# Another order of the SSD stage in a two-layer encoder: taps, softplus, SiLUs and SSD items

## The chip, the cores and the metric

One NeuronCore of one Trainium2 chip runs the whole program. The metric is the device time of one execution in microseconds (us); the time before is the median of three runs, 1902.2 us (1900.9 to 1903.83).

## What is computed

The reference is a trunk of two layers on a sequence of 1024 positions with 1024 channels, float32. Layer 0 is dilated attention, layer 1 a bidirectional Mamba-2 mixer (SSD). Each sub-layer is RMSNorm, shift and scale from `c`, the mixer, a gate and a residual. The part that matters here is the mixer of layer 1, cut to its core (32 heads of 64, 8 groups, state 128, convolution over 5 positions, chunks of 128):

```python
proj = h @ w_in
z, xbc, dt_raw = split(proj)                 # 2048, 4096, 2 x 32
xbc = silu(conv5(xbc) + conv_b)              # depthwise, five taps
xs, bm, cm = split(xbc)                      # 2048, 8 x 128, 8 x 128
dt = softplus(dt_raw + dt_bias)
a = -exp(a_log)
y_f = ssd_scan(xs, dt[:, :, 0], a[0], bm, cm)
y_b = flip(ssd_scan(flip(xs), flip(dt[:, :, 1]), a[1], flip(bm), flip(cm)))
y = (y_f + y_b + xs * d_skip) * silu(z)
return rms_norm(y, norm_w) @ w_out
```

In `ssd_scan`, with `acs` the cumulative sum of `dt * a` in a chunk, the output of a chunk is `(C B^T * decay) (x dt)`, with `decay = exp(acs_l - acs_s)` below the diagonal, plus `exp(acs) * (C state)`, and the states go from chunk to chunk.

## The kernel before

Everything lies transposed: channels on the 128 partitions, positions along the free axis. A float32 product is made of three matmuls on rounded halves (lines 376 to 378). For that each weight tile is loaded by SP into `wraw` (four buffers, line 349), ScalarE rounds it to `whi` (line 271) and VectorE, or GpSimd for a while, subtracts to get `wlo` (line 272, `split`).

The work of layer 1 goes by eight groups g of four heads. A group has six **blocks** of 128 output channels: x0, x1, B, C (convolved) and z0, z1 (gates). A block is eight dense **steps** (`dense`), one per 128 input channels, six matmuls of 512 columns each; it fills two of four accumulator banks `acc`. So a block can start once the banks of the block before the last are free. `block_order` gives the order: x0, z0, x1, B, C, z1 in groups 1 to 6, x0, x1, B, C, z0, z1 in groups 0 and 7. In group 0, x0 and x1 are computed by `start1` together with dt, and B goes to banks `a2`, `a3`.

After a convolved block ScalarE evacuates the middle tap with the bias (line 1322) and VectorE adds the other four taps straight from the banks, two instructions each (line 1330). The banks are free after the last tap. Then comes a SiLU over the tile (line 1334). A gate is evacuated by SiLU or by a copy with a SiLU later (lines 1342, 1347). `group_dense` writes a group's dense steps as a list, with taps and SiLUs inserted behind given steps; the keys of `late` are (position of the block, step).

`dt_items` is the softplus of group 0's head: `tok` transposes dt and takes exp; `ratio`, seven times `series` and `end` compute log1p by a series on VectorE; `rows` makes the cumulative sums by matmuls with triangles and writes them to DRAM (`acsd`); `back` transposes them back and makes `dtdec` (the weights of x for the states). Between `tok` and `back` the splits are GpSimd's.

`ssd_items` gives a group's SSD work, for chunks c of 128 positions: `A1` transposes x0, x1 and B of a chunk (banks `a0`, two of them) and copies them out on ScalarE; `A2` scales x by `dtdec` (xd, line 1415), makes the state products and carries the states; `B0` loads a chunk's `acs` from DRAM into one of four buffers; `B1` makes the exponents E (line 1440), the product cb of B and C, and exp on ScalarE; `M` combines them to the matrices (lines 1462 to 1467); `B2` multiplies and adds x times d (yt, line 1482), and GpSimd multiplies by the gate. B1 of chunk 7 to M of chunk 0 is called the B phase below, the A2 the A phase.

`layer1` joins the lists. A group's SSD items may start at its `cut`, some entries behind the SiLU of B; what follows, up to the next group's cut, is the main list, and `balance` puts the SSD items between its entries so that the estimated VectorE work (fourth number of an entry) keeps up with the estimated TensorE work (third number). `weave` spreads one list over another by its first number. The items of group 7 are woven into its last dense steps and the first 14 steps of the output projection (`out1`).

Of the kernel before, what the change touches and what calls it, by code (L numbers as in the profile page):

```python
# [91 lines left out]
class Trunk:  # L92
# [1097 lines left out]
    def layer1(self, tail):  # L1190
        nc, io = self.nc, self.io
        self.grp, self.ready = {}, {}
        g0 = self.group_dense(0)
        weave(g0[0], tail)
        self.phase("w2")
        self.cv = self.u("cv", [P, 32, 6])
        nc.sync.dma_start(self.cv, io["cv"])
        self.sv = self.u("sv", [P, 34])
        nc.sync.dma_start(self.sv, io["sv"][:, :34])
        self.alog = self.big()[:, :64]  # L1200
        nc.sync.dma_start(self.alog, io["sv"][:, 34:98])
        self.yd = self.scratch("yd", [14, P, S])
        for _, f in g0[1]:
            f()
        main = [g0[2]] + [self.group_dense(g) for g in range(1, 8)]
        cut = [next(i for i, it in enumerate(m) if it[1] is self.ready[g]) + 4 for g, m in enumerate(main)]
        cut[0] += 3
        weave(main[0][:cut[0]], self.dt_items())
        for g in range(7):
            balance(main[g][cut[g]:] + main[g + 1][:cut[g + 1]], self.ssd_items(g))  # L1210
        return main[7][cut[7]:], self.ssd_items(7)
# [6 lines left out]
    def dt_items(self):  # L1218
# [5 lines left out]
        C = 8  # L1224
# [31 lines left out]
        def series(k):  # L1256
            nc.vector.scalar_tensor_tensor(st["q"], st["q"], 1.0 / k, st["w"], op0=OP.add, op1=OP.mult)
# [34 lines left out]
        def back():  # L1292
            self.lo_engine = nc.vector
            p = self.bank("a0", [P, C, 64], 2)
            for c in range(C):
# [7 lines left out]
            nc.vector.tensor_mul(self.dtdec, x, self.dt)  # L1303

        wait = (lambda: None)
        return ([(100, tok), (300, ratio)] + [(200, lambda k=k: series(k)) for k in range(15, 1, -2)]
                + [(300, end), (3800, wait), (100, rows), (1200, wait), (100, back), (3000, wait)])

    def group_dense(self, g):

# [43 lines left out]
        tiles, late, evacs = {}, {}, {}  # L1354
        for pos, m in enumerate(order):
            name = names[m]
            if m < 4:
                e, taps, silu = conv(name, 4 * g + m)
                for i, tp in enumerate(taps):
                    late.setdefault((2, 3 + i) if g == m == 0 else (3 if g == 0 and m == 1 else pos + 1, (0, 1, 3, 5)[i]),  # L1360
                                    []).append(tp)
                if mixed:
                    when = (5, 6) if m == 3 else (5, 0)
                else:
                    when = (5, 0) if m == 3 else (4, 0 if g else 3)
                late.setdefault(when, []).append(silu)
                if m == 2:
                    self.ready[g] = silu[1]
            else:
                e, silu = gate(name, m == 5 or not mixed)  # L1370
                if mixed and m == 4:
                    late.setdefault((5, 1), []).append(silu)
            evacs[m] = e
            banks = ("a2", "a3") if g == 0 and m == 2 else None
            if g or m > 1:
                tiles[pos] = self.dense(self.wb["in1"] + 2 * (6 * g + pos), e, banks)
# [9 lines left out]
    def ssd_items(self, g):  # L1386
# [3 lines left out]
        C = 8  # L1390
# [3 lines left out]
        def ck(c):  # L1394
            return slice(P * c, P * c + P)
# [4 lines left out]
        def A1(c):  # L1400
            p = self.bank("a0", [P, 3, P], 2)
            for i, n in enumerate(("x0", "x1", "B")):
                nc.tensor.transpose(p[:, i], st[n][:, ck(c)], ident)  # L1403
            x = xt[c] = self.u("xt", [P, 4, 64], F32, 8)
            nc.scalar.copy(x.rearrange("p h q -> p (h q)"), p[:, :2].rearrange("p i q -> p (i q)"))
            b = bt[c] = self.u("bt", [P, P], F32, 8)
            nc.scalar.copy(b, p[:, 2])
# [20 lines left out]
        def B0(c):  # L1428
            a = live["a", c] = self.u("acs", [P, 2, 4, P], F32, 4)
            nc.sync.dma_start(a, self.acsd[c, :, hs][None].to_broadcast([P, 2, 4, P]))  # L1430
# [60 lines left out]
                    nc.gpsimd.dma_start(self.yd[2 * g + r], st[f"z{r}"])  # L1491

        def a1(c):
            return 200, lambda: A1(c), 0.35, 0.3

        def a2(j):
            return 900, lambda: A2(j), 0.9, 2.3

        items = []
        for j in range(C // 2):  # L1500
            items += [a1(j), a1(C - 1 - j)]
            if j:
                items.append(a2(j - 1))
        items.append((1, lambda: B0(C - 1), 0, 0))
        items += [a2(j) for j in range(C // 2 - 1, C)]
        if g == 7:
            items.append((1500, lambda: None, 0, 0))
        for c in range(C - 1, -1, -1):
            items.append((900, lambda c=c: B1(c), 0.25, 1.6))
            if c < C - 2:  # L1510
                items.append((500, lambda c=c: B2(c + 2), 1.7, 0.6))
            if c:
                items.append((1, lambda c=c: B0(c - 1), 0, 0))
            items.append((1150, lambda c=c: M(c), 0, 3.0))
        items += [(500, lambda: B2(1), 1.7, 0.6), (900, lambda: None, 0, 1.5), (500, lambda: B2(0), 1.7, 0.6)]
        return items

# [270 lines left out]
```

## Time and profile before

| | |
|---|---|
| median of three runs | 1902.2 us (1900.9 to 1903.83) |
| profiled execution | 1903.41 us, span 1901.6 us |
| TensorE (PE) busy | 1790.2 us, 94% |
| VectorE (DVE) busy | 1428.1 us, 75% |
| ScalarE (ACT) busy | 955.5 us, 50% |
| GpSimd (POOL) busy | 330.1 us, 17% |
| mean granted TensorE clock | 0.976 |

The profile is one execution. A wait is the idle time of an engine just before an instruction, put down to what ended it. A busy TensorE isn't one at its peak, since matmuls are pipelined. The SSD stage with its head lies between about 937 and 1745 us of the span; what goes on before and after it (attention, the projections) is touched by no part of the change.

### The profile page before, as it was taken

What the parts mean: (1) busy time and instruction counts of PE and PEld (TensorE: products, weight loads), DVE (VectorE), ACT (ScalarE), POOL (GpSimd) and SP (SyncE); (2) the same over time, 40 slices, a digit from 0 to 9 for tenths busy, and PEclk for the clock granted to TensorE, in tenths of its full rate; (3) what the DMA queues carried; (4) which work ended last, traced back from release to release, by engine and by line L of the source; (5) the groups of instructions that cost most, each with busy time, mean ns of one, the idle gap of its engine ahead of it and who ended that gap; (6) DMA issues with size and microseconds to landing.
All of it is one profiled execution on the core that took longest, in us unless ns stands there. A gap on an engine that the chain in (4) does not pass through costs nothing.

```text
span 1901.6 us, 28474 instructions
## 1 busy us (share of the span) xinstructions
PE 1790.2 (94%) x10050; PEld 1462.0 (77%) x10050; DVE 1428.1 (75%) x3220; ACT 955.5 (50%) x2095; POOL 330.1 (17%) x492
## 2 busy tenths in 40 slices
PE   5899999999999999999979999999999999888997
PEld 3678788777788887779868887878787877666787
DVE  8867568667664665566778898989898989878875
ACT  5454445444454545444435656464655555465632
POOL 4611122112211311000100101010101000233310
PEclk7899999999999999999989999999999999988998
DMA  6242234222311321355113232424232323244643
GB/s 254 87 130 81 81 107 134 85 86 83 105 52 54 81 60 49 91 188 169 63 45 99 85 100 78 100 78 101 78 110 80 106 83 91 89 129 127 199 155 101
DMA packets 99733, 193.65 MB, mean 102 GB/s; under 512 B 15624, under 2 KB 23048, under 8 KB 99592
## 3 DMA queue, kind: packets, MB, share of 16 engines
q1 hardware_dynamic: 86600, 167.32, 28.3%
q0 software_dynamic: 12288, 23.86, 4.5%
q8 instruction: 79, 1.29, 0.3%
q10 hardware_dynamic: 704, 0.66, 0.1%
q14 instruction: 62, 0.51, 0.1%
HBM read 169.00 MB, written 16.48 MB: 98 GB/s over the span
## 4 chain that ended last, share of the span: by engine, by line
PE 40%; DVE 7%; ACT 5%; issue 3%; DMA 2%; SPq 0%; DVEq 0%; POOL 0%; ACTq 0%; POOLq 0%
PE acc L376 8%; PE acc L378 7%; PE acc L377 7%; PE a L1478 3%; PE a L1416 2%; PE a L1002 2%; PE a L1000 2%; PE a L1001 2%; PE acc L1002 2%; PE acc L1001 1%; PE acc L1000 1%; DVE big L1330 1%; DVE wlo L272 1%; PE a L1403 1%; DMA acs<-acsd 1%
## 5 line engine op out<-in xcount | busy, mean ns | idle before, releaser
L376 PE MATMUL acc<-big,whi 128*128 128x512 f32 (+1 forms) x1520 | 632.7, 416 | 36.2 <-DVE big L1330 23.9
L377 PE MATMUL acc<-big,whi 128*128 128x512 f32 (+1 forms) x1520 | 597.3, 393 | 4.0 <-DVE big L294 4.0
L378 PE MATMUL acc<-big,wlo 128*128 128x512 f32 (+1 forms) x1520 | 597.2, 393 | 0.3 <-DVE wlo L272 0.3
L376 PEld LDWEIGHTS acc<-big,whi 128*128 128x128 f32 x1520 | 289.0, 190 | 103.7 <-issue 31.5
L378 PEld LDWEIGHTS acc<-big,wlo 128*128 128x128 f32 x1520 | 288.6, 190 | 64.8 <-DVE wlo L272 1.1
L377 PEld LDWEIGHTS acc<-big,whi 128*128 128x128 f32 x1520 | 290.1, 191 | 55.3 <-DVE big L294 7.5
L272 DVE TENSOR_TENSOR wlo<-wraw,whi 128x512 fp32r<-128x512 f32 (+1 forms) x298 | 216.8, 732 | 82.3 <-ACT whi L271 78.9
L271 ACT CAST whi<-wraw 128x512 fp32r<-128x512 f32 (+1 forms) x302 | 180.9, 611 | 86.1 <-PE a L1001 29.7
L695 ACT ACTIVATE sm<-sm,nb 128x256 f32<-128x256 f32 (+1 forms) x192 | 89.3, 466 | 198.3 <-DVE nb L693 195.7
L1448 ACT ACTIVATE E<-E,nacb 128x128 f32<-128x128 f32 x256 | 81.8, 391 | 200.2 <-DVE E L1440 200.2
L1486 POOL TENSOR_TENSOR big<-big,yt 128x128 f32<-128x128 f32 x128 | 68.0, 552 | 602.5 <-DVE yt L1482 547.5
L1330 DVE SCALAR_TENSOR_TENSOR big<-acc,cv,big 128x512 f32<-128x512 f32 (+1 forms) x248 | 170.9, 742 | 0.9 <-ACT big L1322 0.9
L706 DVE COPY pt<-a 128x512 f32<-128x512 f32 (+1 forms) x96 | 57.6, 600 | 76.5 <-PE a L704 76.5
L690 DVE CUSTOM_DVE_ANT_0 sm<-a,cst 128x256 f32<-128x256 f32 (+1 forms) x192 | 65.0, 376 | 62.4 <-PE a L685 62.0
L1001 PE MATMUL acc<-big,whi 128*128 128x512 f32 x224 | 91.4, 408 | 9.7 <-DVE big L1553 7.2
L1000 PE MATMUL a<-big,whi 128*128 128x256 f32 (+1 forms) x304 | 100.1, 329 | 0.0
L1002 PE MATMUL a<-big,wlo 128*128 128x256 f32 (+1 forms) x304 | 98.7, 325 | 0.7 <-DVE wlo L272 0.7
L1001 PE MATMUL a<-big,whi 128*128 128x256 f32 (+1 forms) x304 | 98.5, 324 | 0.0
L1002 PE MATMUL acc<-big,wlo 128*128 128x512 f32 x224 | 91.8, 410 | 4.6 <-DVE wlo L272 4.4
L1000 PE MATMUL acc<-big,whi 128*128 128x512 f32 x224 | 92.7, 414 | 1.2 <-ACT big L271 1.2
L592 POOL DMA_DIRECT2D rt<-kT x92 | 50.4, 561 | 249.4 <-ACT kT L532 149.9
L1462 DVE SCALAR_TENSOR_TENSOR W<-cb,dt,W 128x128 f32<-128x128 f32 x256 | 82.7, 379 | 7.3 <-ACT W L1450 6.6
(254 smaller groups left out, 3149.0 us busy)
## 6 DMA issues: line engine op xcount, KB each, us to landing
wraw<-in_win SPq DMA_DIRECT2D x186, 256.0 KB
acs<-acsd SPq DMA_DIRECT2D x64, 512.0 KB
wraw<-in_wout SPq DMA_DIRECT2D x112, 256.0 KB
big<-in_modw SPq DMA_DIRECT2D x48, 512.0 KB
yd<-big POOLq DMA_DIRECT2D x14, 512.0 KB, 3.5
big<-yd SPq DMA_DIRECT2D x28, 256.0 KB
vT<-mix POOLq DMA_DIRECT2D x20, 256.0 KB, 5.0
big<-in_xT SPq DMA_DIRECT2D x8, 512.0 KB
```

The lines of the kernel that those rows point to most:

```text
L271: self.nc.scalar.copy(dst_hi, src)
L272: self.late.append((lambda: self.lo_engine.tensor_sub(dst_lo, src, dst_hi.bitcast(F32)), tile))
L376: mm(o, hi[:, cols], x_[:, t0:t0 + n], start=first, stop=False, **kw)
L377: mm(o, hi[:, cols], x_[:, H2 + t0:H2 + t0 + n], start=False, stop=False, **kw)
L378: mm(o, lo[:, cols], x_[:, t0:t0 + n], start=False, stop=last, **kw)
L695: nc.scalar.activation(sm[:, h, :W], sm[:, h, :W], AF.Exp, bias=nb[:, h:h + 1], scale=0.125, accum_out=stat[:, h, 1, i:i + 1])
L1000: mm(o, hi[:, c], x[:, t:t + n], start=kt == 0 and (n == H2 or m % 2 == 0), stop=False, **kw)
L1001: mm(o, hi[:, c], x[:, H2 + t:H2 + t + n], start=False, stop=False, **kw)
L1002: mm(o, lo[:, c], x[:, t:t + n], start=False, stop=kt == nkt - 1, **kw)
L1330: nc.vector.scalar_tensor_tensor(y[:, lo:hi], a[:, lo + o:hi + o], w[:, cv, k:k + 1], y[:, lo:hi], op0=OP.mult, op1=OP.add)
L1448: nc.scalar.activation(E[:, h], E[:, h], AF.Exp, bias=self.nacb[:, c, 4 * g + h:4 * g + h + 1])
L1462: nc.vector.scalar_tensor_tensor(W[:, h], cb[:, 1], self.dt[:, c, hh:hh + 1], W[:, h], op0=OP.mult, op1=OP.add)
```

## The change

It changes the order of instructions in layer 1 and nothing else.

- `layer1`: a group's SSD items may start 7 entries behind B's SiLU, not 4 (7 in group 0).
- `dt_items`: other first numbers, by which the softplus parts are spread over group 0's dense steps.
- `group_dense`: the four taps of a block go behind steps 0, 1, 2, 3 of the next block, not 0, 1, 3, 5. In group 0 x0's taps go behind steps 0 and 1 of B, x1's behind steps 5 to 7 of B and 0 of C, C's behind steps 0 to 3 of z0, B's behind steps 4 to 7 of z0. Group 0's SiLUs move to step 0 of z1. z0's SiLU in groups 1 to 6 moves from step 1 to step 6 of z1, that of C from 6 to 5.
- `ssd_items`: A1 counts 0.8 instead of 0.3 us of VectorE; the loads B0 of chunks 7 and 6 are issued together ahead of the last A2, and each later one comes behind M, two chunks ahead of its use instead of one.

```diff
         main = [g0[2]] + [self.group_dense(g) for g in range(1, 8)]
-        cut = [next(i for i, it in enumerate(m) if it[1] is self.ready[g]) + 4 for g, m in enumerate(main)]
-        cut[0] += 3
+        cut = [next(i for i, it in enumerate(m) if it[1] is self.ready[g]) + 7 for g, m in enumerate(main)]
...
-        return ([(100, tok), (300, ratio)] + [(200, lambda k=k: series(k)) for k in range(15, 1, -2)]
-                + [(300, end), (3800, wait), (100, rows), (1200, wait), (100, back), (3000, wait)])
+        return ([(200, wait), (100, tok), (100, ratio), (500, wait)]
+                + [(80, lambda k=k: series(k)) for k in range(15, 1, -2)]
+                + [(100, end), (300, wait), (100, rows), (200, wait), (100, back), (700, wait)])
...
-                    late.setdefault((2, 3 + i) if g == m == 0 else (3 if g == 0 and m == 1 else pos + 1, (0, 1, 3, 5)[i]),
-                                    []).append(tp)
+                    if g:
+                        when = pos + 1, i
+                    else:
+                        when = ((2, i // 2), (2 + i // 3, (5, 6, 7, 0)[i]), (4, 4 + i), (4, i))[m]
+                    late.setdefault(when, []).append(tp)
                 if mixed:
-                    when = (5, 6) if m == 3 else (5, 0)
+                    when = (5, 5) if m == 3 else (5, 0)
                 else:
-                    when = (5, 0) if m == 3 else (4, 0 if g else 3)
+                    when = (5, 1) if m == 3 else (4, 0) if g else (5, 0)
...
                 if mixed and m == 4:
-                    late.setdefault((5, 1), []).append(silu)
+                    late.setdefault((5, 6), []).append(silu)
...
-            return 200, lambda: A1(c), 0.35, 0.3
+            return 200, lambda: A1(c), 0.35, 0.8
...
-        items.append((1, lambda: B0(C - 1), 0, 0))
+        items.append((1, lambda: (B0(C - 1), B0(C - 2)), 0, 0))
...
-            if c:
-                items.append((1, lambda c=c: B0(c - 1), 0, 0))
             items.append((1150, lambda c=c: M(c), 0, 3.0))
+            if c > 1:
+                items.append((1, lambda c=c: B0(c - 2), 0, 0))
```

Some lines have other numbers in the changed kernel: from 1208 to 1305 they are one less, from there to 1359 the same, and from the middle of `group_dense` on, the SSD items among it, three more (1403 is 1406, 1440 is 1443).

VectorE at the head of the stage, before. big_8986, big_8984 and big_8985 are tiles of the softplus, big_8958 is x0, and acc_8578 and acc_8579 are its banks:

```order
L272 TENSOR_TENSOR wlo_8919<-wraw_8601,whi_8918 128x512
L1240 COPY big_8986<-a_1636_8975 128x512
L1241 TENSOR_SCALAR big_8984<-big_8986 128x512
L1242 SCALAR_TENSOR_TENSOR big_8984<-big_8986 128x512
L1250 TENSOR_SCALAR big_8985<-big_8984 128x512
L1251 RECIPROCAL big_8985<-big_8985 128x512
L1252 TENSOR_TENSOR big_8984<-big_8984,big_8985 128x512
L1253 TENSOR_TENSOR big_8985<-big_8984 128x512
L1254 TENSOR_SCALAR big_8985<-big_8985 128x512
L1257 SCALAR_TENSOR_TENSOR big_8985<-big_8985 128x512 x7
L1330 SCALAR_TENSOR_TENSOR big_8958<-acc_8578,cv_8789,big_8958 128x512
L1330 SCALAR_TENSOR_TENSOR big_8958<-acc_8579,cv_8789,big_8958 128x510
```

The same place now, from the last tap of x0 on; big_8955 with acc_8580 is x1, and the softplus tiles are big_9012, big_9010 and big_9011:

```order
L1330 SCALAR_TENSOR_TENSOR big_8958<-acc_8578,cv_8789,big_8958 128x510
L1330 SCALAR_TENSOR_TENSOR big_8958<-acc_8579,cv_8789,big_8958 128x512
L272 TENSOR_TENSOR wlo_8980<-wraw_8606,whi_8979 128x512
L1239 COPY big_9012<-a_1639_9001 128x512
L1240 TENSOR_SCALAR big_9010<-big_9012 128x512
L1241 SCALAR_TENSOR_TENSOR big_9010<-big_9012 128x512
L1249 TENSOR_SCALAR big_9011<-big_9010 128x512
L1250 RECIPROCAL big_9011<-big_9011 128x512
L1251 TENSOR_TENSOR big_9010<-big_9010,big_9011 128x512
L1252 TENSOR_TENSOR big_9011<-big_9010 128x512
L1253 TENSOR_SCALAR big_9011<-big_9011 128x512
L1330 SCALAR_TENSOR_TENSOR big_8955<-acc_8580,cv_8789,big_8955 128x512
```

All eight taps of x0 stand ahead of the softplus, and x1's eight between its `ratio` and its `series`; before, x0's were behind the series and x1's behind `end`. On TensorE the matmuls of `rows` follow 20 dense steps of this list, 14 before.

VectorE in the main list of group 1, where x1 of group 2 (big_10748) gets its last taps, before:

```order
L1330 SCALAR_TENSOR_TENSOR big_10748<-acc_10594,cv_8789,big_10748 128x511
L1330 SCALAR_TENSOR_TENSOR big_10748<-acc_10595,cv_8789,big_10748 128x512
L1440 SCALAR_TENSOR_TENSOR E_10840<-acs_10788,delta_8965 128x128 x4
L1446 TENSOR_TENSOR cb_10848<-a_1972_10846,cst_71 128x256
L1482 SCALAR_TENSOR_TENSOR yt_10872<-big_9594,sv_8791,a_1974_10859 128x128
L1482 SCALAR_TENSOR_TENSOR yt_10872<-big_9871,sv_8791,a_1974_10859 128x128
L1462 SCALAR_TENSOR_TENSOR W_10841<-cb_10848,dt_8962,W_10841 128x128 x4
L1464 TENSOR_TENSOR E_10840<-E_10840,W_10841 128x512
L1467 TENSOR_TENSOR acs_10788<-acs_10788,big_10145 128x1024
L1330 SCALAR_TENSOR_TENSOR big_10748<-acc_10594,cv_8789,big_10748 128x510
```

And now:

```order
L1330 SCALAR_TENSOR_TENSOR big_10748<-acc_10594,cv_8789,big_10748 128x510
L1330 SCALAR_TENSOR_TENSOR big_10748<-acc_10595,cv_8789,big_10748 128x512
L272 TENSOR_TENSOR wlo_10843<-wraw_10605,whi_10842 128x512
L1443 SCALAR_TENSOR_TENSOR E_10862<-acs_10751,delta_8965 128x128 x4
L1449 TENSOR_TENSOR cb_10870<-a_1976_10868,cst_71 128x256
L1485 SCALAR_TENSOR_TENSOR yt_10894<-big_9535,sv_8791,a_1978_10881 128x128
L1485 SCALAR_TENSOR_TENSOR yt_10894<-big_9820,sv_8791,a_1978_10881 128x128
L1465 SCALAR_TENSOR_TENSOR W_10863<-cb_10870,dt_8962,W_10863 128x128 x4
L1467 TENSOR_TENSOR E_10862<-E_10862,W_10863 128x512
L1470 TENSOR_TENSOR acs_10751<-acs_10751,big_10107 128x1024
L1330 SCALAR_TENSOR_TENSOR big_10905<-acc_10753,cv_8789,big_10905 128x512
```

The last taps of x1 came behind B1 and M of chunk 2; now those of chunk 2 come behind all of x1's taps, and the next taps are B's (big_10905).

SP's queue where group 7's SSD items begin, before; acs_15829 is the load of chunk 7, acs_16014 that of chunk 6, `yd` are loads for the output projection:

```order
L1430 DMA acs_15829<-acsd 128x2x512
L1530 DMA big_15850<-yd 128x512
L349 DMA wraw_15861<-in_wout 128x512
L1530 DMA big_15880<-yd 128x512
L1530 DMA big_15922<-yd 128x512
L349 DMA wraw_15938<-in_wout 128x512
L1530 DMA big_15971<-yd 128x512
L349 DMA wraw_15979<-in_wout 128x512
L349 DMA wraw_15984<-in_wout 128x512
L1430 DMA acs_16014<-acsd 128x2x512
```

And now:

```order
L1533 DMA big_15837<-yd 128x512
L349 DMA wraw_15847<-in_wout 128x512
L1433 DMA acs_15855<-acsd 128x2x512
L1433 DMA acs_15857<-acsd 128x2x512
L1533 DMA big_15860<-yd 128x512
L1533 DMA big_15902<-yd 128x512
L349 DMA wraw_15929<-in_wout 128x512
L1533 DMA big_15973<-yd 128x512
L349 DMA wraw_15981<-in_wout 128x512
L349 DMA wraw_15986<-in_wout 128x512
```

The load of chunk 6 has moved up past three weight loads, to that of chunk 7, which stands one weight load later.

## Rows read from the trace of the kernel before

**Rows 1.** Busy time by stretch: us of PE, PEld, DVE, ACT, POOL, clock, DMA share, GB/s
```profile
987.00:1080.00 93.00, 92.53 (x552) 76.23 (x550) 77.63 (x168) 53.89 (x124) 6.87 (x15) 1.00 0.29 83
1173.00:1266.00 93.00, 89.56 (x532) 73.23 (x532) 81.72 (x175) 52.44 (x123) 8.81 (x19) 1.00 0.33 91
1266.00:1360.00 94.00, 91.12 (x532) 74.38 (x532) 81.29 (x175) 51.91 (x120) 8.58 (x19) 0.98 0.33 90
```
**Rows 2.** Timeline of TensorE, 946 to 992 us: start, us, instruction, idle before
```profile
948.04 0.39 PE L378 MATMUL a<-big,wlo 128*128 128x512 f32 x1
959.97 0.76 PE L376 MATMUL acc<-big,whi 128*128 128x512 f32 x1 [11.54 <-DVE big L1330]
...
965.65 0.39 PE L376 MATMUL acc<-big,whi 128*128 128x512 f32 x1
...
968.38 0.39 PE L376 MATMUL acc<-big,whi 128*128 128x512 f32 x1
...
988.45 0.99 PE L1403 MATMUL a<-cst,big 128*128 128x128 f32 x6 [0.47 <-ACT bt L1407]
```
**Rows 3.** Timeline of VectorE, 938 to 962 us
```profile
938.72 0.69 DVE L1240 COPY big<-a 128x512 f32<-128x512 f32 x1 [5.14 <-PE a L1236]
...
946.94 6.16 DVE L1257 SCALAR_TENSOR_TENSOR big<-big 128x512 f32<-128x512 f32 x7
953.01 1.40 DVE L1330 SCALAR_TENSOR_TENSOR big<-acc,cv,big 128x512 f32<-128x512 f32 x2
954.33 0.68 DVE L1261 SCALAR_TENSOR_TENSOR big<-big,big 128x512 f32<-128x512 f32 x1
...
956.45 5.35 DVE L1330 SCALAR_TENSOR_TENSOR big<-acc,cv,big 128x512 f32<-128x512 f32 x8
```
**Rows 4.** Timeline of ScalarE, 936 to 942 us
```profile
937.28 2.76 ACT L1322 ACTIVATE big<-acc,cv 128x512 f32<-128x512 f32 x4
```
**Rows 5.** Busy time by short stretches, with the granted clock
```profile
953.40:963.40 10.00, 3.43 (x9) 2.74 (x10) 9.86 (x16) 0.00 (x0) 0.00 (x0) 0.51 0.00 1
...
1243.20:1250.00 6.80, 6.80 (x48) 5.62 (x49) 5.87 (x14) 4.43 (x11) 0.89 (x2) 1.00 0.13 41
...
1629.20:1632.50 3.30, 3.30 (x9) 2.58 (x10) 3.28 (x7) 2.06 (x3) 1.94 (x4) 0.55 0.27 109
```
**Rows 6.** Waits of TensorE, 1173 to 1266 us: total, times, longest
```profile
PE acc L376 <- DVE big L1330: 1.5, 1, 1.5
PE a L1403 <- ACT bt L1407: 1.2, 1, 1.2
PE a L1403 <- ACT big L1334: 0.3, 1, 0.3
```
**Rows 7.** Waits of TensorE, 1545 to 1634 us
```profile
PE acc L376 <- DVE big L1330: 4.7, 3, 1.7
PE a L1478 <- issue: 2.8, 1, 2.8
```
**Rows 8.** Busy time, 1600 to 1630 us
```profile
1600.00:1630.00 30.00, 23.78 (x184) 19.38 (x183) 28.84 (x68) 19.91 (x45) 4.84 (x11) 0.98 0.26 69
```
**Rows 9.** Waits of VectorE, 1634 to 1745 us
```profile
DVE E L1440 <- DMA acs<-acsd: 6.6, 1, 6.6
```
**Rows 10.** Timeline of SP's queue, 1600 to 1760 us
```profile
1633.99 0.67 SPq L1430 DMA_DIRECT2D acs<-acsd  x1
...
1642.40 0.33 SPq L349 DMA_DIRECT2D wraw<-in_wout  x1
...
1663.71 11.73 SPq L349 DMA_DIRECT2D wraw<-in_wout  x2
1675.49 0.43 SPq L1430 DMA_DIRECT2D acs<-acsd  x1
```
**Rows 11.** Timeline of VectorE in a steady group, 1244 to 1254 us
```profile
1244.17 1.13 DVE L1440 SCALAR_TENSOR_TENSOR E<-acs,delta 128x128 f32<-128x128 f32 x4
1245.22 0.41 DVE L1446 TENSOR_TENSOR cb<-a,cst 128x256 f32<-128x256 f32 x1
...
1250.32 1.13 DVE L1462 SCALAR_TENSOR_TENSOR W<-cb,dt,W 128x128 f32<-128x128 f32 x4
...
1252.10 1.22 DVE L1467 TENSOR_TENSOR acs<-acs,big 128x1024 f32<-128x1024 f32 x1
```
**Rows 12.** Timeline of VectorE, 950.3 to 951.6 us: one step of the series
```profile
949.84 1.80 DVE L1257 SCALAR_TENSOR_TENSOR big<-big 128x512 f32<-128x512 f32 x1
```

## The prediction

> **What bounds the kernel now.** I looked first at the busy time by stage. TensorE is the bound: between 987 and 1080 us it worked 92.53 of 93 us, from 1173 to 1266 89.56 of 93, while VectorE had 81.72 [rows 1]. So the only gains to be had are TensorE's waits and the stretches in which its clock was at the lower of its two levels, and I went through the SSD stage wait by wait.
>
> At its head stands the largest. TensorE ended the B block of group 0 at 948.3 and started C at 959.97, 11.54 us later, released by a tap on VectorE [rows 2]. The C block needs the two accumulators of x0, and these come free with x0's taps. VectorE had meanwhile been in the softplus: it copied dt at 938.72, began the series of seven steps at 946.94 and ended them at 953.0; then two taps, the softplus end at 954.33, and the other taps from 956.45 [rows 3]. Yet x0 had been evacuated since 940.04 (four evacuations, from 937.28 on for 2.76 us) [rows 4]. The idle time had a second price: from 953.4 to 963.4 the granted clock was 0.51, which is the 1.2 GHz level, and 3.43 us of that were worked [rows 5], so 1.7 us were lost after the restart.
>
> In the steady groups TensorE waits 3.0 us per group: 1.5 for a tap ahead of a dense block, 1.2 + 0.3 for ScalarE at the transposes A1 [rows 6]. One group has 1.6 us more TensorE time (91.12 against 89.56) at a granted clock of 0.98 [rows 1]. Group 6 waits 4.7 for taps and 2.8 at an SSD matmul [rows 7], but VectorE is busy 28.84 of the 30 us from 1600 to 1630 [rows 8]: there it is the bound. In the last group VectorE itself stood still for 6.6 us, for a load of acs [rows 9]; SP issued the load before it at 1633.99, this one at 1675.49, after a weight load that had held the queue for 11.73 us from 1663.71 [rows 10].
>
> **The change part by part.** The sum goes against the profiled execution, 1903.4 us, of which 1901.6 are span. It lies 1.2 above the median of the runs.
>
> *Head.* Gone: 11.5 of waiting and 1.7 of half rate, 13.2. Now x0's eight tap instructions start at 940.0; eight take 5.3 us (956.45 to 961.7) [rows 3], so they end at 945.3, before B ends at 948.3: C doesn't wait. What is late next is the softplus. After a split of 0.6 its first part takes 8.2 (938.72 to 946.94), to 954.2; x1's taps 5.3, to 959.5; the series 6.1, to 965.6; the end 2.1 (954.33 to 956.45), to 967.7 [rows 3]. TensorE has C done at 948.3 + 8 steps of 1.37 (twelve matmuls in 2.73 us, 965.65 to 968.38) [rows 2] = 959.2. z0 waits 0.3 for x1's taps. By the new order the prefix matmuls of `rows` come after 20 dense steps instead of 14, that is four steps into z0, at 965.0; they need the softplus end, so they wait 2.7. A wait of 1.5 us at 1243 was followed by a granted clock of 1.00, one of 2.8 at 1627.9 by 0.55 over 3.3 us [rows 5, 7]. 2.7 is nearest to the latter, so I take one such stretch, 1.7 us. New: 0.3 + 2.7 + 1.7 = 4.7. Queued behind that wait on TensorE are the rest of z0 and z1; nothing else needs it soon, since dtdec is due only at the first A2, 14 dense steps on. Of the splits of weights, one that GpSimd did is now VectorE's (the 0.6). Head: **-8.5**, with ends at -11 (no loss of clock, and the wait 1.1 shorter) and -5 (the wait 2 longer, the stretch at the lower clock twice as long).
>
> The Trainium skill's "TensorE: Matmul & The Clock Gate", section "HAM oscillation — how this bites in real kernels", has the clock fall only after an idle gap longer than a length that it names, and 2.7 is below that; by it the new cost would be 3.0 and the head -10.2. The wait of 2.8 in the rows was below it too and the clock fell, so I stay with the rows.
>
> *Groups 1 to 5.* All five get the same new order. The wait at the transposes shrinks: A1 now comes four dense steps behind the three SiLUs, and z0's SiLU is out of the way. Four A1 in a row still share two banks; in group 0, with ScalarE free, they cost 0.47 [rows 2]. The wait at the tap: x1's last taps stood behind M of chunk 2; now B1, the yt and M of chunk 2 come after them. That takes 1.5 + 0.5 + 2.9 = 4.9 us of VectorE work (1244.17 to 1245.6, one yt pair, 1250.32 to 1253.23 [rows 11]) from ahead of the block start, against 2 dense steps less of cover (2.7, since B1 of chunk 7 comes after step 8 of the next group instead of after step 6). 1.5 + 2.7 - 4.9 is below 0: no wait. But the 2.7 of cover are missing behind that point: VectorE comes to M of chunk 1, and to the xd products of the next A2, with less slack, and TensorE waits there. Ends: 0 and 3.3 (the 2.7 and a split of 0.6); I take 1.0, between 0 and the 1.5 at which a tap is late now. Gone are five waits of 1.5 for taps, five of 1.5 at the transposes, and 1.6 of clock, 16.6; new are 5 x 0.5 and 5 x 1.0. Groups 1 to 5: **-9.1**, ends -14 and +2.4.
>
> *Group 0* has no wait now except that 0.47 [rows 2]; its SSD items begin seven dense steps later and its B phase has the fewest steps of all, 28: **+2.0**, ends 0 and 3.3.
>
> *Group 6.* VectorE has the same work in about as many steps (30 from B1 of chunk 7 to the last B2, 29 before): **0**, ends -5 and +3.
>
> *Last group.* B0 of chunk 6 is issued together with that of chunk 7, three weight loads earlier in SP's queue than now, and that of chunk 7 one later: both behind the weight load that SP issued at 1642.40, ahead of the one that held it from 1663.71 [rows 10]. So the 6.6 us go; VectorE then meets one split and one prep earlier (1.1). The other loads of acs are at most one weight load earlier, and the four buffers still cover them. VectorE is the bound there, so its gain is TensorE's. **-5.5**, ends 0 and -8. The two dense steps that go from this stage to group 6 cost the same in either place.
>
> Softplus, SiLUs, loads and matmuls are as many as before; the 200 and 80 in the lists are weights, not work. Sum: -8.5 - 9.1 + 2.0 + 0 - 5.5 = -21.1, so 1882.3 against 1903.4, and 1.2 less against the median: **1881 us**.
>
> **Rivals.**
> *The arrears eat the groups.* B phases that VectorE can't finish in 28 to 32 steps put waits of 3.0 and more back into each group. For it: by the prices above the phase has 59 us of VectorE work (8 x 1.5 of B1, 8 x 2.9 of M, 6 x 0.5 of yt, 12 pairs of taps at 1.3, 8 splits at 0.6) against 32 steps, 44 us, and less than half of a group's 24 us of SSD matmuls (89.56 - 48 x 1.37); against it: VectorE idles in the A phase, 81.72 of 93 us busy in the whole group [rows 1]. Then groups 1 to 5 give nothing: -8.5 + 0 + 2 - 5.5 = -12, 1890.
> *TensorE alone bounds.* VectorE's slack suffices everywhere, group 6 included: -11 - 14 - 5 - 8 = -38, 1864. For it: VectorE's 81.72 of 93; against it: group 6's 28.84 of 30.
> *GpSimd holds the series up.* One of the seven series steps took 1.80 us instead of 0.7, beside a split on GpSimd [rows 12]. Until `back` all splits run there, and two more may fall beside the series: 2 x 1.1 more waiting at `rows`, and 1.7 more at the lower clock, +3.9: 1885. The Trainium skill's "SBUF — State Buffer", section "Who interferes with whom", has this as a rule: a VectorE instruction with two SBUF inputs and a GpSimd one that reads SBUF block each other. By that rule the trace agrees: 1.80 is one GpSimd split and one step.
> *Slower.* The arrears stop TensorE at two places per group, at B2 of chunk 1 (M late) and at A2 of chunk 0 (xd behind C's taps), by 3.3 each. Six groups: 39.6 against 16.6 removed there, +23, with the head's and the tail's -14 = +9: 1911. It decides from (16.6 + 14) / 6 = 5.1 us of new waiting per group on. Against it: five dense steps lie between M of chunk 0 and A2, and VectorE is idle 11 us per group.
>
> **How the numbers follow.** A measurement can tell about 0.2%, 3.8 us. Forecast 0.46 (1873 to 1888), arrears 0.20, TensorE-bound 0.15, GpSimd 0.10, slower 0.06, and 0.03 that parts cancel within 0.2%. All but the last two are faster: 0.91. The range leaves out the slow case and the outer half of the TensorE-bound one: 1867 to 1895.
>
> **What would show it.** Right: C starts within 0.5 us of B's end; a wait of 2 to 4 us at `rows`; no wait for taps in groups 1 to 5, their period 90 to 91.5 us instead of 89.6 + 3.0 = 92.6; no VectorE wait for acs in the last group. Wrong: the wait at `rows` is above 5; SSD matmuls wait for acs or E at the end of each B phase by more than 3 us; the last group's VectorE stretch is as long as before.

## The result, and the profile after

The changed kernel takes 1870.1 us (median of 4 runs, 1867.3 to 1870.7) against 1903.0 for the kernel before beside it: ratio 0.983 (95% interval 0.981 to 0.985), 33 us less. Forecast were 1881 us, 21 less. The profiled execution spans 1868.0 us against 1901.6; the stretches below are its own.

Where the 33.6 us of the spans lie, by the starts of the same dense block in both traces (the 2,208 dense matmuls of 512 columns from the head on are all recorded, 48 to a block, so a block is found by counting). At z1 of groups 1 to 6 both kernels have done the same SSD work; at z1 of group 7 the changed one is seven short matmuls, about 1 us, behind, so 1 us of the fifth row belongs to the sixth:

| from, to | before | after | difference | forecast |
|---|---|---|---|---|
| start, B of group 0 | 936.50 | 934.89 | -1.6 | none (no part of the change) |
| B of group 0, z1 of group 1 | 137.29 | 128.79 | -8.5 | head -8.5 and a part of group 0's +2.0 |
| z1 of group 1, z1 of group 2 | 91.07 | 91.93 | +0.9 | the rest of the +2.0 and a fifth of -9.1 |
| z1 of group 2, z1 of group 6 | 372.50 | 357.21 | -15.3 | four fifths of -9.1 |
| z1 of group 6, z1 of group 7 | 111.82 | 106.82 | -5.0 | 0 |
| z1 of group 7, end | 252.46 | 248.38 | -4.1 | -5.5 |

The first row is noise: over all the profiles of this case that block starts between 934.9 and 939.8 us. Of the last row 1.3 us lie behind the last SSD product, where nothing was changed.

TensorE's waits in the whole stage of the changed kernel, 930 to 1760 us (total, times, longest):

```profile
PE a L1481 <- DVE acs L1470: 9.8, 6, 2.7
PE a L1419 <- DVE xd L1418: 5.7, 5, 2.9
PE acc L1001 <- DVE big L1556: 4.3, 3, 2.4
PE a L1273 <- DVE big L1263: 3.1, 1, 3.1
PE a L1406 <- ACT bt L1410: 2.1, 7, 0.3
...
PE acc L376 <- DVE big L1330: 0.7, 1, 0.7
```

The taps (L1330) are left with 0.7 us; before they had the 11.54 of the head [rows 2], 1.5 per group [rows 6] and 4.7 in group 6 [rows 7]. ScalarE at A1 (L1406, before L1403) is left with 0.3 per group, 1.5 before [rows 6]. What remains, besides `rows` (L1273) and the output projection (L1001), is late products of M (L1481 behind L1470), in groups 0, 6 and 7, and xd, nearly all in group 7.

The head on TensorE:

```profile
946.66 0.39 PE L376 MATMUL acc<-big,whi 128*128 128x512 f32 x1
...
958.36 0.47 PE L376 MATMUL acc<-big,whi 128*128 128x512 f32 x1 [0.66 <-DVE big L1330]
...
967.20 3.10 PE L1273 MATMUL a<-cst,big 128*32 128x128 f32 x32 [3.10 <-DVE big L1263]
```

and on VectorE, with a line of GpSimd:

```profile
938.47 5.36 DVE L1330 SCALAR_TENSOR_TENSOR big<-acc,cv,big 128x512 f32<-128x512 f32 x8 [6.50 <-ACT big L1322]
...
950.63 1.78 DVE L1251 TENSOR_TENSOR big<-big,big 128x512 f32<-128x512 f32 x1
...
953.52 5.35 DVE L1330 SCALAR_TENSOR_TENSOR big<-acc,cv,big 128x512 f32<-128x512 f32 x8
958.79 6.02 DVE L1256 SCALAR_TENSOR_TENSOR big<-big 128x512 f32<-128x512 f32 x7
964.84 0.69 DVE L1260 SCALAR_TENSOR_TENSOR big<-big,big 128x512 f32<-128x512 f32 x1
```
```profile
949.34 2.54 POOL L272 TENSOR_TENSOR wlo<-wraw,whi 128x512 fp32r<-128x512 f32 x2 [0.56 <-ACT whi L271]
```

x0's eight taps come first and C starts at 946.66 without a wait [rows 2, 3]; z0 waits 0.66, `rows` 3.10 for the softplus. A product of `ratio` (L1251) took 1.78 us beside two splits on GpSimd; before, without one, it took 0.69 (L1252). Busy time by short stretches (us of PE, PEld, DVE, ACT, POOL, clock, DMA share, GB/s) shows the price behind the second wait, one stretch at the lower level, where before there were 10 us of it [rows 5]:

```profile
967.20:970.30 3.10, 3.10 (x33) 2.72 (x33) 3.10 (x6) 0.58 (x1) 0.00 (x0) 0.60 0.03 5
970.30:974.00 3.70, 3.70 (x14) 2.52 (x14) 3.70 (x7) 2.68 (x12) 0.73 (x1) 0.88 0.37 71
```

A steady group, from 1166 to 1255 us, answers to the second line of [rows 1]: 0.3 us of TensorE idle instead of 3.4, and VectorE idle for 8.7 of the 89 us:

```profile
1166.00:1255.00 89.00, 88.70 (x531) 72.95 (x531) 80.33 (x174) 52.30 (x120) 8.78 (x18) 1.00 0.35 95
```

In the last group VectorE has no wait for acs any more [rows 9], but longer ones for the inputs of the output projection, 7.0 instead of 3.0 us (waits of VectorE, 1634 to 1745 us before, 1605 to 1712 now):

```profile
DVE big L1553 <- ACT big L1552: 3.0, 1, 3.0
```
```profile
DVE big L1556 <- ACT big L1555: 7.0, 3, 3.6
DVE cb L1449 <- PE a L1446: 3.5, 1, 3.5
```

From z1 of group 7 to the last SSD product (before, then now) TensorE is idle for 13.5 us in both kernels; what differs is the granted clock, 0.89 and 0.94:

```profile
1649.20:1741.60 92.40, 78.95 (x427) 60.62 (x425) 79.26 (x151) 50.14 (x114) 31.04 (x25) 0.89 0.38 114
```
```profile
1619.70:1709.30 89.60, 76.12 (x434) 59.34 (x433) 81.29 (x151) 54.28 (x122) 30.75 (x27) 0.94 0.41 120
```

### The profile page after: what moved, and what is told of

Its sections match the earlier page's. It is cut to its first block, busy times and chain, and to the rows that moved or that the text cites. A ratio compares the mean times of both kernels' runs of the same rounds, so it can differ in the third digit from the quotient of the medians.

```text
span 1868.0 us, 28492 instructions
## 1 busy us (share of the span) xinstructions
PE 1781.9 (95%) x10050; PEld 1457.3 (78%) x10050; DVE 1421.3 (76%) x3219; ACT 956.5 (51%) x2095; POOL 327.2 (18%) x493
## 4 chain that ended last, share of the span: by engine, by line
PE 39%; DVE 11%; ACT 3%; DMA 2%; issue 2%; SPq 0%; POOL 0%; DVEq 0%; ACTq 0%; POOLq 0%
PE acc L376 8%; PE acc L378 7%; PE acc L377 7%; PE a L1481 3%; PE a L1419 2%; DVE big L1330 2%; PE a L1000 2%; PE a L1001 2%; PE a L1002 2%; DVE wlo L272 2%; PE acc L1002 1%; PE acc L1000 1%; PE acc L1001 1%; DVE W L1465 1%; DVE acs L1470 1%
## 5 line engine op out<-in xcount | busy, mean ns | idle before, releaser
L695 ACT ACTIVATE sm<-sm,nb 128x256 f32<-128x256 f32 (+1 forms) x192 | 89.3, 466 | 198.8 <-DVE nb L693 196.1
L1330 DVE SCALAR_TENSOR_TENSOR big<-acc,cv,big 128x512 f32<-128x512 f32 (+1 forms) x248 | 169.4, 743 | 6.5 <-ACT big L1322 6.5
L1001 PE MATMUL a<-big,whi 128*128 128x256 f32 (+1 forms) x304 | 97.9, 322 | 0.0
L1001 PE MATMUL acc<-big,whi 128*128 128x512 f32 x224 | 88.8, 396 | 6.1 <-DVE big L1556 4.3
L1002 PE MATMUL acc<-big,wlo 128*128 128x512 f32 x224 | 89.3, 399 | 3.3 <-DVE wlo L272 2.7
L1000 PE MATMUL acc<-big,whi 128*128 128x512 f32 x224 | 90.5, 404 | 1.3 <-ACT big L271 1.2
L1322 ACT ACTIVATE big<-acc,cv 128x512 f32<-128x512 f32 x62 | 44.5, 769 | 86.4 <-PE acc L378 76.1
```

The costliest lines, as they stand in the source:

```text
L695: nc.scalar.activation(sm[:, h, :W], sm[:, h, :W], AF.Exp, bias=nb[:, h:h + 1], scale=0.125, accum_out=stat[:, h, 1, i:i + 1])
L1000: mm(o, hi[:, c], x[:, t:t + n], start=kt == 0 and (n == H2 or m % 2 == 0), stop=False, **kw)
L1001: mm(o, hi[:, c], x[:, H2 + t:H2 + t + n], start=False, stop=False, **kw)
L1002: mm(o, lo[:, c], x[:, t:t + n], start=False, stop=kt == nkt - 1, **kw)
L1330: nc.vector.scalar_tensor_tensor(y[:, lo:hi], a[:, lo + o:hi + o], w[:, cv, k:k + 1], y[:, lo:hi], op0=OP.mult, op1=OP.add)
```

## The experiments

The steady groups gave twice what was forecast, so the first question is which of the parts did it. Four runs put one part each back, with everything else as in the changed kernel.

**Taps back** (`r_taps`):

```diff
-                        when = pos + 1, i
+                        when = pos + 1, (0, 1, 3, 5)[i]
```

> The changed kernel with one thing put back: the taps of groups 1 to 7 behind steps 0, 1, 3, 5 of the next block. Theory 'each part its own wait': the wait for x1's last tap went because the taps' own places moved; put back, 1.7 us per group return (1.5 of waiting and 0.2 of refilling TensorE), and group 6 waits for taps again: 1878 to 1884 us against 1870. Theory 'order against M': the wait went because the SSD items stand later, so that M of chunk 2 comes behind x1's last tap; in this kernel it still does (x1's last tap follows B1 and B2 of chunk 2, M of chunk 2 follows it), so no wait for taps in groups 1 to 5 and at most 2 us in all: 1868 to 1873.

Measured 1874.9 us, ratio 0.986 (0.984 to 0.987). The period of groups 2 to 6 is 89.8 us instead of 89.3, with no wait for a tap in it: the second theory, though the time lies 2 us above its range. The new places of the taps are worth 0.5 us per group there. The two waits for taps that did come back, 2.3 and 3.6 us, are in the B phases of groups 0 and 6.

**SiLUs back** (`r_silu`):

```diff
-                    when = (5, 5) if m == 3 else (5, 0)
+                    when = (5, 6) if m == 3 else (5, 0)
...
-                    late.setdefault((5, 6), []).append(silu)
+                    late.setdefault((5, 1), []).append(silu)
```

> The changed kernel with the SiLU of z0 back at step 1 and that of C back at step 6 of z1 in the mixed groups. Theory 'z0's SiLU ahead of the copies': ScalarE does it before it can copy the first transposes out, so the waits of 1.2 to 1.5 us at A1 come back, 2.0 us per group with the refill, six times: 1880 to 1884. Theory 'the transposes stand later': A1 still comes four dense steps behind the three SiLUs, which is enough for a fourth one of 0.7 us; A1 waits 0.3 as in the changed kernel: 1868 to 1873.

Measured 1885.0, ratio 0.991 (0.989 to 0.993): 1 us above the range of the first theory, but without its wait. A1 waits 0.3 as in the changed kernel; TensorE waits at the last SSD product (waits of a steady group):

```profile
PE a L1481 <- issue: 1.8, 1, 1.8
```

**Start of the SSD items back** (`r_cut`):

```diff
+        cut = [c - 3 * (g > 0) for g, c in enumerate(cut)]
```

> The changed kernel with the SSD items of groups 1 to 7 allowed 4 entries behind B's SiLU again, not 7. Theory 'z0's SiLU ahead of the copies': A1 now follows the SiLUs of x0, x1 and B two dense steps sooner, but z0's SiLU is still out of the way: waits at A1 below 0.6 per group, 1868 to 1874. Theory 'the transposes stand later': the waits of 1.2 to 1.5 at A1 come back, 2.0 us per group: 1880 to 1884.

Measured 1892.4, ratio 0.995 (0.993 to 0.997), worse than either theory, and again without waits at A1. The steady groups have periods of 92.0, and group 6 is 7 us longer. VectorE and TensorE of a steady group show the place:

```profile
1252.13 1.36 DVE L1466 SCALAR_TENSOR_TENSOR W<-cb,dt,W 128x128 f32<-128x128 f32 x4
1253.53 0.69 DVE L1468 TENSOR_TENSOR E<-E,W 128x512 f32<-128x512 f32 x1
1254.14 0.69 DVE L1471 TENSOR_TENSOR acs<-acs,big 128x512 f32<-128x512 f32 x1
```
```profile
1254.92 0.44 PE L1482 MATMUL a<-acs,SS 128*64 128x128 f32 x4 [2.10 <-issue]
```

That is M of chunk 0 and its product, B2 of chunk 0, the last of the group. The wait is put down to "issue", but the product starts 0.09 us behind the end of M's last instruction (1254.14 + 0.69). The product of chunk 1 waits 0.9 us for its M there too. In the changed kernel the same two stand so:

```profile
1250.32 0.69 DVE L1470 TENSOR_TENSOR acs<-acs,big 128x512 f32<-128x512 f32 x1
```
```profile
1252.27 0.44 PE L1481 MATMUL a<-acs,SS 128*64 128x128 f32 x4
```

The product has 1.26 us to spare. By the written order of groups 1 to 5 three dense steps stand between M of chunk 0 and its product in the changed kernel, one in the kernel before, in `r_cut` and in `r_silu`.

**Count of A1 back** (`r_a1w`):

```diff
-            return 200, lambda: A1(c), 0.35, 0.8
+            return 200, lambda: A1(c), 0.35, 0.3
```

> The changed kernel with A1 counted as 0.3 us of VectorE again instead of 0.8: four A1 of a group follow one another sooner and the whole of a group's SSD items after them comes one or two dense steps earlier. Theory 'the copies bound A1': four A1 in a row wait for ScalarE's copies, 1.2 us and a refill of 0.8 per group: 1880 to 1884. Theory 'cover decides': the B phase gets one or two more steps, the waits for M in group 0 (1.9) and group 6 (4.7) shrink and nothing comes at A1 (0.5 at most per group): 1864 to 1869.

Measured 1879.1, ratio 0.987 (0.985 to 0.989): slower, against 'cover decides', and not by A1, which waits 0.3. The product follows M directly here and waits 1.0 per group:

```profile
PE a L1481 <- issue: 1.0, 1, 1.0
```

So in the steady groups the start of the SSD items, the SiLUs and the count of A1 act by one thing, the end of the B phase. Counted in the written order of groups 1 to 5, with the waits and mean periods of groups 2 to 6:

| kernel | dense steps from B1 of chunk 7 to M of chunk 0 | from there to its product | TensorE waits for M | period |
|---|---|---|---|---|
| changed, `r_taps` | 32 | 3 | none | 89.3, 89.8 |
| `r_silu` | 32 | 1 | 1.8 | 91.9 |
| `r_cut` | 32 | 1 | 2.1 and 0.9 | 92.0 |
| `r_a1w` | 35 | 0 | 1.0 | 90.9 |
| before | 34 | 1 | none (1.5 for a tap, 1.5 at A1) | 93.1 |

The second and third row have as many steps ahead of M as the changed kernel, and two fewer behind it. `r_a1w` has none behind it, but three more ahead, and waits less: both sides of M count.

A probe of that place (`p_none`), with a pause of the planner ahead of the last product taken out:

```diff
-        items += [(500, lambda: B2(1), 1.7, 0.6), (900, lambda: None, 0, 1.5), (500, lambda: B2(0), 1.7, 0.6)]
+        items += [(500, lambda: B2(1), 1.7, 0.6), (900, lambda: None, 0, 0), (500, lambda: B2(0), 1.7, 0.6)]
```

> The changed kernel with the pause ahead of a group's last SSD product (B2 of chunk 0), 1.5 us in the planner's count of VectorE, counted as 0. That product then stands right behind M of chunk 0, and M itself two to three dense steps later. Theory 'distance to the last product': TensorE waits for M there, a chain of 3.5 us on VectorE, in each of seven groups: 3 us each with its refill, 1885 to 1892. Rival 'the later the SSD items the better': 1866 to 1872.

Measured 1936.9, ratio 1.019 (1.017 to 1.021). The direction is that of the first theory, the price three times mine: periods of 98.5 to 99.0 instead of 89.3, and in a steady group

```profile
PE a L1481 <- DVE yt L1485: 7.3, 1, 7.3
```

since M of chunk 0 had itself moved behind three of C's four taps on VectorE. So the probe changes more than the distance. VectorE itself stood still for 3.60 us ahead of M, at a split whose weight ScalarE rounded only behind a table load and three SiLUs, and behind the wait the granted clock was 0.50 for 4.4 us:

```profile
1273.09 0.69 DVE L272 TENSOR_TENSOR wlo<-wraw,whi 128x512 fp32r<-128x512 f32 x1 [3.60 <-ACT whi L271]
```
```profile
1277.70:1282.10 4.40, 4.37 (x22) 3.59 (x23) 2.21 (x6) 0.00 (x0) 2.73 (x6) 0.50 0.00 2
```

Then the three parts alone on the kernel before (`o_three`; of the last three edits only the lines put in):

```diff
-        cut[0] += 3
+        cut = [c + 3 for c in cut]
...
+                    when = (5, 5) if m == 3 else (5, 0)
...
+                    late.setdefault((5, 6), []).append(silu)
...
+            return 200, lambda: A1(c), 0.35, 0.8
```

> The kernel before with three things of the change alone: the SSD items of groups 1 to 7 allowed 7 entries behind B's SiLU, the SiLUs of z0 and C at steps 6 and 5 of z1, and A1 counted as 0.8. Taps, softplus and the loads of acs stay as before. Theory 'these three make the steady groups': the periods from z1 to z1 of groups 2 to 6 come from 92.7 down to 89.5 to 90, and the time is 1880 to 1886. Rival 'taps, loads or the head have a share in the steady groups': periods of 91 and more, 1888 to 1896.

Measured 1878.4, ratio 0.987 (0.985 to 0.989), 2 us under the expectation. Groups 2 to 6 have periods of 89.8, as with the taps put back. These three are enough for the steady groups, and for 24.5 of the 33 us.

**The other two parts put back.** The head (`r_head`), that is the list of `dt_items` and group 0's places of taps and SiLUs as before:

> The changed kernel with the head put back: the softplus parts, the taps and the SiLUs of group 0 as before. The head of the kernel before took 8.5 us more up to z1 of group 1; the group after it took 91.9 us in the changed kernel against 89.3 in the later ones, 2.6 more. Theory 'group 0's arrears come from its late SSD items': with the old head they start seven dense steps sooner, so the 2.6 go as the 8.5 come: 1875 to 1877. Rival 'the arrears come from the order of the steady groups and meet the first group anyway': 1877.5 to 1880.

Measured 1880.5, ratio 0.989 (0.987 to 0.990). Up to z1 of group 1 it is 9.2 us longer, and the next period 89.9 instead of 91.9: 2.0 of the 2.6 us go, as the first theory has it. The time lies above its range. In the profile 1.2 us came on ahead of B of group 0, where the edit alters nothing, and 2.5 behind z1 of group 6, where it alters one thing (the SiLU of C in group 7 has its place from the same line as in group 0, and goes back by one dense step); 1876.6 to 1880.8 was the spread of the runs.

The loads of acs (`r_b0`):

```diff
-        items.append((1, lambda: (B0(C - 1), B0(C - 2)), 0, 0))
+        items.append((1, lambda: B0(C - 1), 0, 0))
...
+            if c:
+                items.append((1, lambda c=c: B0(c - 1), 0, 0))
             items.append((1150, lambda c=c: M(c), 0, 3.0))
-            if c > 1:
-                items.append((1, lambda c=c: B0(c - 2), 0, 0))
```

> The changed kernel with the loads of acs put back to one chunk ahead, each before M. Theory 'the load bounds the last group': VectorE waits about 6 us for acs at the head of the last group's B phase again and the last group is 4 to 6 us longer: 1874 to 1876. Rival 'the last group is bound by VectorE's work, the wait was cover': 1868 to 1872. The steady groups show no change either way.

Measured 1872.8, ratio 0.985 (0.983 to 0.986), between the two. VectorE's wait for acs in the last group is 2.4 us, not 6, and in `o_three`, which has the old loads too, 0.6 (waits of VectorE in the last group, `r_b0` and `o_three`):

```profile
DVE E L1443 <- DMA acs<-acsd: 2.4, 1, 2.4
```
```profile
DVE E L1440 <- DMA acs<-acsd: 0.6, 1, 0.6
```

SP's queue in `o_three` shows why:

```profile
1648.61 6.20 SPq L349 DMA_DIRECT2D wraw<-in_wout  x2
...
1655.82 0.42 SPq L1430 DMA_DIRECT2D acs<-acsd  x1
```

The weight loads ahead of that of chunk 6 still hold SP, but for 6.20 us instead of 11.73 [rows 10], and the load is only 0.6 us late.

The six runs that put a part back lose 64 us between them, twice what the change gave: each moves the whole order, so its loss is not the price of its part.

**Could the order be better still?** `rows` three steps later (`n_rows`):

```diff
-                + [(100, end), (300, wait), (100, rows), (200, wait), (100, back), (700, wait)])
+                + [(100, end), (650, wait), (100, rows), (200, wait), (100, back), (350, wait)])
```

> The changed kernel with the prefix matmuls of the softplus (rows) three dense steps later, behind 23 instead of 20, and back behind 26. Theory 'a moved wait': the 3.1 us of waiting there and the 1.7 us of the lower clock behind it go, and nothing else is late: 1864 to 1866.5. Rival 'VectorE owes the time anyway': TensorE reaches group 0's B phase sooner and waits there for M instead: 1868 to 1871.

Measured 1868.7, ratio 0.984 (0.982 to 0.985), no difference from the changed kernel that can be told. The wait at `rows` is gone and z1 of group 1 comes 3.4 us sooner, but the next period is 1.1 us longer, 93.0: TensorE still waits for M in group 0's B phase, 2.07 us where the changed kernel had 1.94, and now the clock falls behind that wait (timeline, and busy time with 0.51 as the clock):

```profile
1065.76 1.12 PE L1481 MATMUL a<-acs,SS 128*64 128x128 f32 x8 [2.07 <-DVE acs L1470]
```
```profile
1065.70:1069.20 3.50, 3.44 (x26) 3.05 (x27) 3.43 (x12) 2.63 (x9) 0.92 (x2) 0.51 0.22 75
```

So group 0's items were started two steps sooner as well (`n_cut0`: `cut[0] -= 2`, and weights 600, 200, 250 in the list above):

> The run before with rows three steps later, and besides the SSD items of group 0 two entries (two dense steps) sooner, so that its B phase has the cover of the later groups. Theory 'group 0 owes two steps': the period from z1 of group 1 to z1 of group 2 comes from 93.0 down to 89.3 to 90.0, and with the 3.4 us that rows gave in the head the time is 1863 to 1866. Rival 'VectorE has a fixed debt from the softplus': TensorE then waits for xd at the first A2 or at the transposes instead, 1867 to 1871.

Measured 1870.5, ratio 0.983 (0.981 to 0.985). The period is 89.6, as expected; but ScalarE now stood in the way, at A1:

```profile
986.26 1.54 PE L1407 MATMUL a<-cst,big 128*128 128x128 f32 x6 [3.61 <-ACT bt L1411]
```

Its exponent of `back` had slid in among the SiLUs, with a table load of 1.28 us (L1302, 981.49) ahead of it and one (L1335, 983.43) behind:

```profile
981.49 1.28 ACT L1302 ACT_TABLE_LOAD   x1
982.78 0.63 ACT L1302 ACTIVATE big<-big 128x512 f32<-128x512 f32 x1
983.43 1.28 ACT L1335 ACT_TABLE_LOAD   x1
```

The last version (`n_silu0`) moves x0's and x1's SiLU of group 0 to where ScalarE is idle, C's behind four A1, and `back` ahead of the rest (the lines put in):

```diff
+        cut[0] -= 3
...
+                + [(100, end), (450, wait), (100, rows), (50, wait), (100, back), (450, wait)])
...
+                    when = (5, 1 if g else 4) if m == 3 else (4, 0) if g or m < 2 else (5, 0)
```

> The changed kernel with group 0 ordered anew: rows behind 22 dense steps and back behind 23, the SiLUs of x0 and x1 at the start of z0 (ScalarE is idle there), C's behind the first four A1, and the SSD items two dense steps sooner. In the run before, ScalarE did the SiLUs of x0, x1, B and C and loaded its function tables three times between 974 and 985 us, and A1 waited 3.6 us for its copies. Theory 'ScalarE's chain of exponent and SiLUs holds the transposes': with two SiLUs gone from it A1 waits less than 2 us, and of the 4.8 us at rows and the 2.6 of group 0's debt about 4 remain as a gain: 1864 to 1867. Rival 'the softplus on VectorE sets the head's end whatever stands behind': A1 waits 3 us and more again, 1868 to 1871.

Measured 1865.4 (1861.8 to 1867.1), ratio 0.981 (0.979 to 0.983). TensorE's waits from 930 to 1100 us come to 2.4 us, where `n_cut0` had 4.6, and the clock from 937 to 988 is 1.00:

```profile
PE a L1407 <- ACT big L1335: 0.7, 1, 0.7
PE acc L376 <- DVE big L1331: 0.7, 1, 0.7
PE a L1407 <- ACT bt L1411: 0.6, 2, 0.3
PE a L1274 <- DVE big L1264: 0.4, 1, 0.4
```

Up to z1 of group 7 it takes 5.5 us less than the changed kernel (679.3 against 684.8 from B of group 0). The two were not timed beside each other, and the intervals of their ratios overlap.

A miss: the first four preparations of the output projection four steps later (`n_prep`):

```diff
-                m.insert(len(m) - 10 + 2 * i, (1, lambda i=i: prep(0, i)))
+                m.insert(len(m) - 6 + 2 * i if i < 3 else len(m), (1, lambda i=i: prep(0, i)))
```

> The changed kernel with the four preparations of the first output-projection inputs (prep) four dense steps later in the last group. VectorE stood still 7.0 us there for ScalarE's half of them, and TensorE 5.4 us for xd behind them. Theory 'the preparations hold xd up': TensorE waits less than 2 us for xd, and the VectorE-bound stretch behind starts 4 to 6 us sooner: 1864 to 1867. Rival 'VectorE's B phase is bound by its start, M of chunk 7': the idle time moves behind the A phase, 1868 to 1872.

Measured 1873.2, ratio 0.985 (0.983 to 0.987). TensorE's wait for xd stays at 5.5 us: VectorE waits for the same preparations at another place.

## Why the prediction was right, and where it was off

**Head.** Right, step by step: C without a wait, 0.66 at z0 (0.3 forecast), 3.1 at `rows` (2.7), one stretch at the lower clock. The Trainium skill's "TensorE: Matmul & The Clock Gate", section "HAM oscillation — how this bites in real kernels", warns only of longer idle gaps than this one of 3.1 us; here the clock fell behind it. One split on GpSimd fell beside the series, as in the sum (6.02 us, 6.1 forecast); others fell beside `ratio` and cost 1.1 us there, which the sum did not have and which is enough for the longer wait at `rows`. From B of group 0 to x0 of group 1 it is 56.0 us instead of 71.0; 6.4 of that are SSD matmuls which now come later, so the head gave about 8.7 (8.5 forecast).

**Group 0.** +2.0 was forecast for its shorter B phase; the period behind it is 2.6 us longer than the later ones, and `r_head` gets 2.0 of that back.

**Groups 1 to 5.** The sign was right, the size was half: -9.1 forecast, -17.1 measured (-15.3 in the fourth row and, for group 1, 91.07 less the later period of 89.3), which is outside the ends given, -14 and +2.4; the period of 89.3 lies below the 90 to 91.5 named as the sign. The step that failed is the sum's new waits of 0.5 and 1.0 per group, 7.5 us in all, which did not come. I had counted what the new order takes from VectorE's cover in the middle of the B phase, and missed what it adds at its end, three dense steps ahead of the last product instead of one. `r_cut`, `r_silu` and `r_a1w` show that a group's time is then decided at this end. A smaller error goes the same way: a wait costs more than its idle time. The period from 1164.85 (before) became 3.7 us shorter, for waits that shrank by 3.1 (1.53 for the tap, 1.54 at A1); what the rest is, no run takes apart. That the tap wait hung on the order against M held (`r_taps`). Neither the taps' steps nor the start of the SSD items brings that order alone: with either put back M of chunk 2 still comes behind x1's last tap, and no wait for taps returns in these groups (`r_taps`, `r_cut`).

**Group 6.** 0 forecast in a range of -5 to +3, -4.0 measured (the fifth row less its 1 us). From z1 of group 6 to z1 of group 7 TensorE's waits fell from 12.0 to 8.4 us: the taps' 4.7 went, those at A1 fell from 1.8 to 0.8 and those for xd from 2.7 to 1.8, while those for M grew from 2.8 to 5.8 (4.7 and 1.1). The stretch at the lower clock at 1629 [rows 5], 1.7, didn't return, which may be chance (see the last section). That makes 5.3, of which 1.3 were lost again where no run shows. VectorE was the bound there only in part.

**Last group.** -5.5 forecast, -5.1 measured, and that they lie so close is luck. VectorE's wait for acs went, but the step from there, that VectorE's gain is TensorE's, did not hold: TensorE stands still as long as before, in other places, and what went is time at the lower clock, 1.3 us of it behind the last SSD product. Nor was it the loads' own move: in `o_three`, with the old loads, acs is nearly in time, since the steps ahead of it had moved, and the way from z1 of group 7 to the end takes 246.4 us, less than in the changed kernel. `n_silu0`, `n_cut0` and `n_rows`, whose written order from there on is that of the changed kernel, took 249.0, 250.9 and 252.8 where it took 248.4 and the kernel before 252.5; so how much of the last row belongs to the change is not shown. Put back alone the loads cost 2.7 us, with intervals that overlap.

**The rivals.** "TensorE alone bounds" gave 1864, and the 1870 measured lie between it and the forecast, nearer to it, and below the 1873 to 1888 that the forecast's chance of 0.46 was for: groups 1 to 5 went past its -14, group 0 stayed short of it. "The arrears" was wrong for groups 1 to 5 and right for group 0. The slower case needed 5.1 us of new waiting per group; `p_none`, with 7.3, shows that it was there to be had, at the end of the B phase, not at the two places named. "GpSimd" came true in part: 1.1 us once, and no second stretch at the lower clock. Two counts in the prediction are one off and change nothing: by the written order six dense steps, not five, lie between M of chunk 0 and the next group's A2, and group 0's B phase has 27 up to M, not 28.

Open: which of the three parts took away the waits at A1. With any one put back A1 still waits 0.3 at most, but there TensorE has just stood still at the last product, which may give ScalarE the time.

## What to carry to other kernels

When one list of work is put between the steps of another, look first at the last item of each round, and count the steps on both sides of its producer: here two steps less behind it cost 2.6 us of a round of 89, other places of the taps in the middle 0.5. Moving one part of such a plan moves others; count the steps between producer and consumer for every pair in the woven order, not for the part that the diff names. Price a removed wait above its idle time (here 3.7 for 3.1), and a wait moved elsewhere at its full price until the new place has been looked at.

## What the runs showed of the hardware

The length of a wait alone did not tell whether the clock fell. In the changed kernel a wait of 2.66 us at 1600.55 was followed by 1.00, one of 2.02 at 1701.17 by 0.57. Nor did the written order: seven kernels have the same order in group 6 (but for the loads of acs in `r_b0`) and the same wait for M, 2.66 to 2.69 us. Behind it the clock was 1.00 in three (changed, `n_rows`, `n_prep`) and 0.57 to 0.64 over 3.5 us in four (`r_head`, `r_b0`, `n_cut0`, `n_silu0`), so 1.7 us between two single profiles can be this alone. The changed kernel, and then `n_cut0`:

```profile
1600.50:1604.00 3.50, 3.45 (x33) 2.97 (x34) 3.50 (x11) 3.23 (x10) 0.88 (x2) 1.00 0.00 0
...
1701.10:1705.10 4.00, 3.93 (x28) 3.34 (x29) 4.00 (x10) 2.00 (x7) 1.73 (x4) 0.57 0.18 66
```
```profile
1600.80:1604.30 3.50, 3.44 (x27) 3.05 (x28) 3.50 (x11) 3.21 (x10) 0.87 (x2) 0.57 0.00 0
```

In every kernel here some waits of a product for M stand under "issue", and each of these products started 0.10 us behind M's end; such a row is to be read against the producer's own timeline.
